# A hybrid decoder trunk on one core: two decay tables bound behind the delta branch's inputs, and one group of transposes behind its last product

## The chip, the cores and the metric

The kernel runs on one core of a Trainium2 chip. The core has a matrix engine (TensorE, PE in the profile, with its weight loads under PEld), a vector engine (VectorE, DVE), an activation engine (ScalarE, ACT), a general engine (GpSimd, POOL) and a queue engine (SyncE, SP) that issues most of the transfers. Each engine runs its own list of instructions in order, and the lists meet only in semaphores. The metric is the time of one execution in microseconds, as the median of several.

## The reference, cut to what matters

The reference has two layers. Each is a half-step feed-forward block, a token-mixing part with two branches side by side, and another half-step feed-forward block. All sizes are small in tokens (256) and large in channels (1024), in float32.

```python
for l in range(DEPTH):                                  # DEPTH = 2
    h = h + 0.5 * swiglu(rms_norm(h, ffn1_norm[l]), ffn1_w_in[l], ffn1_w_out[l])
    u = rms_norm(h, mix_norm[l])
    (z_s, xbc, dt_s, qkv, z_d, b_d, a_d, gate_s, gate_d) = jnp.split(u @ w_in[l], split_points, axis=-1)
    y_s = mamba2_branch(z_s, xbc, dt_s, ...)            # the state branch, 4 groups of 8 heads
    y_d = deltanet_branch(qkv, z_d, b_d, a_d, ...)      # the delta branch, 8 heads
    merged = (jax.nn.sigmoid(gate_s) * (y_s @ ssm_w_branch[l])
              + jax.nn.sigmoid(gate_d) * (y_d @ dn_w_branch[l]))
    h = h + merged @ w_out[l]
    h = h + 0.5 * swiglu(rms_norm(h, ffn2_norm[l]), ffn2_w_in[l], ffn2_w_out[l])
return rms_norm(h, final_norm)
```

In the state branch a chunk of 128 tokens is weighted by `cb * decay`, where `decay` is the exponential of a difference of running sums, one 128 by 128 table for each head and chunk:

```python
seg = a_cum[:, :, :, None] - a_cum[:, :, None, :]
decay = jnp.where(causal, jnp.exp(jnp.where(causal, seg, 0.0)), 0.0)
y_diag = jnp.einsum("bclsg,bclsgh,bcsghp->bclghp", cb, decay, xdt)
```

## The kernel before, in words

Every weight matrix is streamed once from memory in tiles of 128 by 1024 (`wraw`). To keep float32 accuracy at the matrix engine's fast rate, ACT rounds each tile to a high part (`whi`, L68) and DVE takes the rest (`wlo`, L71). A product then is three matmuls: high by high, high by low, low by high. There are five buffers each for `wraw`, `whi` and `wlo`; a buffer is free again when the last reader of the tile in it is done, so the preparation runs up to five tiles ahead of PE and no more.

The mixer is a list of steps, `ORDER`, in which the code is written; a scheduler that works on estimated times then lays the instructions of each engine into one list, and within that it may move an instruction ahead of an older one. The steps that the change is about are the last third of the list: `D0 S0 x10 T0 D1 x11 g110 g111 S1 x20 T1 o x21 N D2 y S2 D3 x30 x31 T2 g000 g010 g001 S3 g011 T3`.

- `Dg` is `decay(g)`: the decay table of group g, `dc`, 128 by 2048. A transfer spreads the running sums over the partitions (L1061), DVE subtracts (`dc<-dc,ac`), clips at zero (L78), ACT takes the exponential, and DVE multiplies with the masked products of the group (`dc<-dc,cbt`). Two buffers, `sA` and `sB`, alternate between the groups.
- `xgi` is `xs_unit`: a product of 48 matmuls of 256 columns into one of four accumulator banks (`xs`), and then for each of its halves a convolution of width 4: one ACT instruction that writes `ca`, three DVE instructions on `ca` (255, 254 and 253 columns, L74) that read the bank, and a Silu on ACT that writes `xsT`. The bank is free when the last of these has read it.
- `Sg` is the first part of `ssd(g)`: eight transposes of `xsT` on PE (`xsb`, L1101), then on DVE the tiles `xD`, `xdt` and `xe`. `Tg` is the rest: 32 small products with the decay table (`ydb`, L1115) and one more (`yob`), sums on DVE (`xD`, `yo`), the gating by `yz`, a Square with a sum on ACT (`jk`, `sss`), a reciprocal root on POOL (`srr`, L210), and two scalings by it on ACT (`yz<-yz,srr`).
- `g...` are gate products: 24 matmuls of 512 columns into two banks (`t0`, `t1`).
- `o` and `N` are the delta branch's end. `dn_T(hp)` transposes four heads' outputs on PE (`oT`, L1154), gates them on DVE (`og`), and splits them into a high part on ACT (`bh`) and a low part on DVE (`bl`). `dn_branch` multiplies these with the branch's weights in 96 matmuls of 512 columns (`b`, L335 to L337) into four banks, and adds to the gates (`tg`).
- `y` is `ss_T(0)`, four transposes (`yT`, L1169) of the state branch's first group, whose product follows after `T3`.

`tc.issue_after(ins)` binds the instructions that a block writes behind `ins` on the engine of `ins`, if they are on that engine. It makes no semaphore; it only fixes their place in that engine's list.

Of the kernel before, what the change touches and what calls it, by code (L numbers as in the profile page):

```python
# [11 lines left out]
ALU = mybir.AluOpType  # L12
# [4 lines left out]
P = 128  # L17
D = 1024
S = 256
# [34 lines left out]
def trunk_kernel(ctx, tc, x, wst, wsm, norms, lpar, rpar, cst, out):  # L54
    nc = tc.nc
    V, A, G, PE = nc.vector, nc.scalar, nc.gpsimd, nc.tensor
# [10 lines left out]
    def act(o, i, func=AF.Copy, **kw):  # L67
        return A.activation(out=o, in_=i, func=func, **kw)  # L68

    def tt(o, a, b, op):  # L70
        return V.tensor_tensor(out=o, in0=a, in1=b, op=op)  # L71

    def stt(o, a, s, b, op0, op1):
        return V.scalar_tensor_tensor(out=o, in0=a, scalar=s, in1=b, op0=op0, op1=op1)  # L74

    def ts(o, a, s1, op0, sc2=None, op1=None):
        if op1 is None:
            return V.tensor_scalar(out=o, in0=a, scalar1=s1, scalar2=None, op0=op0)  # L78
        return V.tensor_scalar(out=o, in0=a, scalar1=s1, scalar2=sc2, op0=op0, op1=op1)

    def f(ap):
        return ap.bitcast(F32)

    def tmp2(name):
        return s2.tile([P, 512], F32, tag="s2", name=name)

    def trb(name):
        return trp.tile([P, 512], F32, tag="tr", name=name)

    def accb(name):  # L90
        return accp.tile([P, 512], F32, tag="acc", name=name)

    def small(shape, name, bufs=2):
        return sm.tile(shape, F32, tag=name, name=name, bufs=bufs)
# [54 lines left out]
    state = {"loaded": 0, "prepped": 0, "taken": 0, "last": None, "hold": False, "behind": {}, "late": {}, "first": 0, "turns": {}, "first_chunk": False, "cap": n_forms}  # L149
# [69 lines left out]
    h = cpool.tile([P, 2, D], F32, name="h")  # L219
# [11 lines left out]
    ident = cs[:, 0:P]  # L231
# [164 lines left out]
    def out_chunks(ps, stat, ks, last, group=1, split=False, first=None):  # L396

        for g0 in range(0, len(ks), group):
            kk = ks[g0 : g0 + group]
            ws = [(k, take()) for k in kk]  # L400
            for t in range(2):
                order = [(k, n) for n in range(2) for k in range(len(kk))]
                if t == 1 and not split:
                    m = len(kk) - 2 if len(kk) == NSPL else len(kk)
                    order = [(k, n) for k in range(m) for n in range(2)]
                    order += [(k, n) for n in range(2) for k in range(m, len(kk))]
                order = [(k, n, 0, 512) for k, n in order]
                if t == 1 and split:
                    order = [o for o in order if o[1] == 0]
                    order += [(k, 1, c, c + 256) for c in (0, 256) for k in range(len(kk))]  # L410
                state["sums"] = []
                for k, n, c0, c1 in order:
                    k, (wh, wl) = ws[k]
                    sh, sl = stat(k, t)
                    c = slice(n * 512 + c0, n * 512 + c1)
                    begin = k == 0 if first is None else first and t == n == 1
                    bank = ps[t][n][:, c0:c1]
                    if c0:
                        begin, bank = k == kk[0], ps[2][:, 0:256]
                    ins = mm3(bank, sh, sl, wh[:, c], wl[:, c], begin, k == last)  # L420
                    state["sums"].append(ins)
# [171 lines left out]
    def mixer(l, nxt):  # L593
# [13 lines left out]
        yz = {}  # L607
# [37 lines left out]
        ac = small([P, 2, 40], "ac", 1)  # L645
# [380 lines left out]
        late = {}  # L1026
# [32 lines left out]
        def decay(g):  # L1059
            dc = slots.tile([P, 8, 2, P], F32, tag=("sA", "sB")[g % 2], name="dc")  # L1060
            nc.sync.dma_start(  # L1061
                dc[:].rearrange("p h t l -> p (h t l)"),
                rdram[8 * g : 8 * g + 8].rearrange("a b -> (a b)").partition_broadcast(P),
            )
            tt(
                dc[:], dc[:],
                ac[:, :, 8 * g : 8 * g + 8].rearrange("p t h -> p h t")[:, :, :, None].to_broadcast([P, 8, 2, P]),
                ALU.subtract,
            )
            dv = dc[:].rearrange("p h t l -> p (h t l)")  # L1070
            ts(dv, dv, 0.0, ALU.min)
            act(dv, dv, AF.Exp)
            tt(dc[:], dc[:], late["cbm"][:, g, None].to_broadcast([P, 8, 2, P]), ALU.mult)
            decs[g] = dc

        def xs_unit(g, i):
# [73 lines left out]
        def dn_T(hp):  # L1150
            bank = trb("oT")
            bv = bank[:].rearrange("p (a c i) -> p a c i", a=2, c=4)
            for c in range(4):
                PE.transpose(bv[:, :, c, :], vb[:, c, hp, :], ident)  # L1154
            og = tmp2("og")
            stt(og[:], bank[:], dnw, late["zdT"][:, 2 * hp : 2 * hp + 2, :].rearrange("p h t -> p (h t)"), ALU.mult, ALU.mult)
            oh = s2.tile([P, 2, S], F32R, tag="s2", name="bh")
            ol = s2.tile([P, 2, S], F32R, tag="s2", name="bl")
            act(oh[:].rearrange("p a t -> p (a t)"), og[:])
            tt(ol[:].rearrange("p a t -> p (a t)"), og[:], f(oh[:]).rearrange("p a t -> p (a t)"), ALU.subtract)  # L1160
            brT[("d", hp)] = (oh, ol)

        def ss_T(j):
            bank = trb("yT")
            g, k0 = j // 2, (j % 2) * 2
            for k in range(2):
                for t in range(2):
                    c0 = (k0 + k) * P
                    PE.transpose(bank[:, k * S + t * P : k * S + (t + 1) * P], yz[g][:, t, c0 : c0 + P], ident)  # L1169
            oh = s2.tile([P, 2, S], F32R, tag="s2", name="bh")  # L1170
            ol = s2.tile([P, 2, S], F32R, tag="s2", name="bl")
            for k in range(2):
                w = snw[:, 2 * j + k : 2 * j + k + 1]
                act(oh[:, k], bank[:, k * S : (k + 1) * S], scale=w)
                stt(ol[:, k], bank[:, k * S : (k + 1) * S], w, f(oh[:, k]), ALU.mult, ALU.subtract)
            brT[("s", j)] = (oh, ol)

        def branch(kind, n, mk, tail=1):
            ps = [[accb("b"), accb("b")] for _ in range(2)]
            held = {}  # L1180

            def stat(k, t):
                oh, ol = held[k // 2]
                return oh[:, k % 2, t * P : (t + 1) * P], ol[:, k % 2, t * P : (t + 1) * P]

            made = 1
            for j0 in list(range(n - tail)) + [n - tail]:
                js = range(j0, j0 + (tail if j0 == n - tail else 1))
                while made < min(js[-1] + 2, n):
                    mk(made)  # L1190
                    made += 1
                for j in js:
                    held[j] = brT.pop((kind, j))
                out_chunks(ps, stat, [2 * j + i for j in js for i in range(2)], 2 * n - 1, group=2 * len(js))
            return ps

        def dn_branch():
            ps = branch("d", 4, dn_T)
            m = tg[1]
            for t in range(2):  # L1200
                for n in range(2):
                    sl = slice(n * 512, (n + 1) * 512)
                    stt(m[:, t, sl], m[:, t, sl], 1.0, ps[t][n][:], ALU.add, ALU.mult)
# [5 lines left out]
        def step(name):  # L1209
# [10 lines left out]
            elif kind == "M":  # L1220
                masks()
            elif kind == "I":
                next(inv, None)
            elif kind == "R":
                next(rc, None)
            elif kind == "b":
                bcm(*num)
            elif kind == "d":
                zdm(*num)
            elif kind == "x":  # L1230
                xs_unit(*num)
            elif kind == "P":
                drain(ssd_pre())
            elif kind == "D":
                decay(*num)
            elif kind == "g":
                gate(*num)
            elif kind == "S":
                heads[num[0]] = ssd(*num)
                next(heads[num[0]])  # L1240
            elif kind == "T":
                drain(heads[num[0]])
            elif kind == "o":
                dn_T(0)
            elif kind == "y":
                ss_T(0)
            elif kind == "N":
                dn_branch()
# [33 lines left out]
    for l in range(DEPTH):  # L1282
        ffn(norm_vec(3 * l + 1))
        mixer(l, 3 * l + 2)
        add = ffn(norm_vec(3 * l + 3) if l + 1 < DEPTH else None)
# [153 lines left out]
```

## Time and profile before

| what | value |
|---|---|
| median of 3 runs | 1543.27 us (1543.04 to 1545.02) |
| the profiled execution's own time | 1541.48 us |
| its span from first to last instruction | 1539.7 us |
| granted TensorE clock | 0.999 |
| DVE busy / ACT busy | 1229.7 us (80%) / 944.8 us (61%) |
| memory read | 297.72 MB, 195 GB/s over the span |

Each row of the timeline gives the start and the length of an instruction, or of a run of equal ones, in microseconds, then the engine, the line, the operation, the tiles (written `<-` read), the sizes and the count; in brackets stands how long the engine had been idle before it, and who released it. An engine starts its next instruction a little before the former has ended, so the step from start to start is somewhat shorter than the length. The two layers run the same lists: the first layer's mixer ends its state branch at about 404 to 572 us, and the second's some 761 us later.

### The profile page before, as it was taken

The numbers are of one execution on the slowest core, as the hardware profiler recorded it, in microseconds if no ns is written. First come the engines' busy times: TensorE is split into PE (matmuls) and PEld (weight loads), VectorE is DVE, ScalarE is ACT, GpSimd is POOL, SyncE is SP. The second block draws the span as 40 slices with busy tenths as digits, with TensorE's granted clock in tenths as the row PEclk, the third lists the DMA queues.
The fourth block names the chain that finished last, engine by engine and source line by source line (L and its number), as shares of the span: only waits on it lengthen the run. The fifth ranks groups of instructions, "written<-read, shape, count | busy, mean of one in ns | idle before, by whom it ended". The sixth has DMA issues, their size and how long they took to land.

```text
span 1539.7 us, 29072 instructions
## 1 busy us (share of the span) xinstructions
PE 1522.8 (99%) x11473; PEld 1384.4 (90%) x11473; DVE 1229.7 (80%) x1859; ACT 944.8 (61%) x1532; POOL 81.8 (5%) x92
## 2 busy tenths in 40 slices
PE   8999999999999999999999999999999999999998
PEld 7999889999888888999899998899998888899997
DVE  6878769967899766789778887689589996677886
ACT  5655667765665645555555566676756666455565
POOL 0000110000000000000100012010000000000010
PEclk9999999999999999999999999999999999999999
DMA  7687775653565556587867687665345555556785
GB/s 277 190 265 231 226 228 167 187 164 111 178 213 171 163 166 196 185 256 211 261 225 225 208 253 229 197 193 180 117 141 202 179 170 186 176 177 195 247 241 156
DMA packets 98831, 305.73 MB, mean 199 GB/s; under 512 B 22837, under 2 KB 23813, under 8 KB 97670
## 3 DMA queue, kind: packets, MB, share of 16 engines
q1 hardware_dynamic: 93796, 290.95, 57.2%
q0 software_dynamic: 4608, 12.58, 5.1%
q8 instruction: 90, 1.47, 0.4%
q14 instruction: 47, 0.39, 0.1%
q10 hardware_dynamic: 290, 0.33, 0.1%
HBM read 297.72 MB, written 1.92 MB: 195 GB/s over the span
## 4 chain that ended last, share of the span: by engine, by line
PE 89%; DVE 4%; ACT 2%; DMA 2%; issue 1%; SPq 1%; POOL 0%; POOLq 0%; ACTq 0%; DVEq 0%
PE fc L346 10%; PE fc L340 9%; PE fc L345 9%; PE t L366 9%; PE o L337 4%; PE o L335 4%; PE o L336 4%; PE f L366 3%; PE b L335 3%; PE b L337 3%; PE b L336 3%; PE p L336 2%; PE p L337 2%; PE p L335 2%; PE xs L345 1%; PE xs L340 1%
## 5 line engine op out<-in xcount | busy, mean ns | idle before, releaser
L71 DVE TENSOR_TENSOR wlo<-wraw,whi 128x1024 fp32r<-128x1024 f32 x488 | 591.8, 1221 | 186.7 <-ACT whi L68 172.2
L68 ACT ACTIVATE whi<-wraw 128x1024 fp32r<-128x1024 f32 x488 | 511.6, 1059 | 271.0 <-PE fc L345 92.5
L346 PE MATMUL fc<-uW,wlo 128*128 128x256 f32 x1280 | 354.9, 277 | 0.0
L340 PE MATMUL fc<-uW,whi 128*128 128x256 f32 x1280 | 354.1, 277 | 0.0
L345 PE MATMUL fc<-uW,whi 128*128 128x256 f32 x1260 | 348.3, 276 | 0.0
L340 PEld LDWEIGHTS fc<-uW,whi 128*128 128x128 f32 x1280 | 240.5, 188 | 0.8
L346 PEld LDWEIGHTS fc<-uW,wlo 128*128 128x128 f32 x1280 | 240.5, 188 | 0.0
L345 PEld LDWEIGHTS fc<-uW,whi 128*128 128x128 f32 x1260 | 236.5, 188 | 0.8
L366 PE MATMUL t<-whi,uW 128*128 128x512 f32 x512 | 165.3, 397 | 0.0
L366 PEld LDWEIGHTS t<-whi,uW 128*128 128x128 f32 x512 | 95.9, 188 | 21.6 <-issue 1.3
L68 ACT ACTIVATE whi<-wsum 128x1024 fp32r<-128x1024 f32 x64 | 68.0, 1062 | 58.8 <-PE fc L345 32.9
L366 PE MATMUL t<-wlo,uW 128*128 128x512 f32 x256 | 100.2, 392 | 0.0
L71 DVE TENSOR_TENSOR wlo<-wsum,whi 128x1024 fp32r<-128x1024 f32 x64 | 78.2, 1221 | 7.9 <-ACT whi L68 5.6
L335 PE MATMUL b<-whi,bh 128*128 128x512 f32 x192 | 76.1, 398 | 0.3
L336 PE MATMUL b<-wlo,bh 128*128 128x512 f32 x192 | 74.9, 390 | 0.0
L337 PE MATMUL b<-whi,bl 128*128 128x512 f32 x192 | 74.2, 393 | 0.0
L340 PE MATMUL xs<-uW,whi 128*128 128x256 f32 x256 | 72.8, 284 | 0.0
L346 PE MATMUL xs<-uW,wlo 128*128 128x256 f32 x256 | 71.4, 279 | 0.0
L345 PE MATMUL xs<-uW,whi 128*128 128x256 f32 x254 | 70.6, 278 | 0.0
L335 PE MATMUL o<-whi,gh 128*128 128x512 f32 (+1 forms) x160 | 62.0, 388 | 0.0
L337 PE MATMUL o<-whi,gl 128*128 128x512 f32 (+1 forms) x160 | 61.8, 386 | 0.0
L336 PE MATMUL o<-wlo,gh 128*128 128x512 f32 (+1 forms) x160 | 61.7, 386 | 0.0
(337 smaller groups left out, 3291.7 us busy)
## 6 DMA issues: line engine op xcount, KB each, us to landing
wraw<-in_wst_dram SPq DMA_DIRECT2D x504, 512.0 KB, 4.9
wsum<-in_wst_dram SPq DMA_DIRECT2D x16, 512.0 KB, 7.3
wsum<-in_wst_dram POOLq DMA_DIRECT2D x16, 512.0 KB, 8.7
dc<-rdram SPq DMA_DIRECT2D x8, 1024.0 KB, 8.5
nw<-in_norms_dram SPq DMA_DIRECT2D x6, 512.0 KB, 5.9
h<-u POOLq DMA_DIRECT2D x12, 256.0 KB, 6.8
gb<-rdram SPq DMA_DIRECT2D x8, 256.0 KB, 5.6
h<-in_x_dram SPq DMA_DIRECT2D x4, 256.0 KB, 3.7
```

The source lines that it names most:

```text
L68: return A.activation(out=o, in_=i, func=func, **kw)
L71: return V.tensor_tensor(out=o, in0=a, in1=b, op=op)
L335: PE.matmul(ps, lh, rh, start=start, stop=False)
L336: PE.matmul(ps, lh, rl, start=False, stop=False)
L337: return PE.matmul(ps, ll, rh, start=False, stop=stop)
L340: PE.matmul(ps, wh, mh, start=start, stop=False)
L345: PE.matmul(ps, wh, ml, start=False, stop=False)
L346: PE.matmul(ps, wl, mh, start=False, stop=stop)
L366: ins = PE.matmul(ps[t][:], st, mv, start=k0 == 0 and j == 0, stop=k0 == KT - 2 and j == 5)
```

## The change

The third and the fourth group's decay table are touched: for g of 2 and 3, `decay(g)` puts its subtraction on DVE behind an instruction kept in `late["branch"]`. For the third group that is the low part of the delta branch's last heads (`bl` of hp 3); for the fourth it is the third group's last multiplication, because `decay` now also stores its own last instruction there. And the four transposes of `ss_T(0)` are bound on PE behind the last product of the delta branch.

```diff
-            tt(
-                dc[:], dc[:],
-                ac[:, :, 8 * g : 8 * g + 8]...to_broadcast([P, 8, 2, P]),
-                ALU.subtract,
-            )
+            with ExitStack() as behind:
+                if g > 1:
+                    behind.enter_context(tc.issue_after(late["branch"].ins))
+                tt(
+                    dc[:], dc[:],
+                    ac[:, :, 8 * g : 8 * g + 8]...to_broadcast([P, 8, 2, P]),
+                    ALU.subtract,
+                )
...
-            tt(dc[:], dc[:], late["cbm"][:, g, None].to_broadcast([P, 8, 2, P]), ALU.mult)
+            late["branch"] = tt(dc[:], dc[:], late["cbm"][:, g, None].to_broadcast([P, 8, 2, P]), ALU.mult)
...
-            tt(ol[:].rearrange("p a t -> p (a t)"), og[:], f(oh[:]).rearrange("p a t -> p (a t)"), ALU.subtract)
+            ins = tt(ol[:].rearrange("p a t -> p (a t)"), og[:], f(oh[:]).rearrange("p a t -> p (a t)"), ALU.subtract)
             brT[("d", hp)] = (oh, ol)
+            if hp == 3:
+                late["branch"] = ins
...
-                    PE.transpose(bank[...], yz[g][:, t, c0 : c0 + P], ident)
+                    with ExitStack() as behind:
+                        if j == 0:
+                            behind.enter_context(tc.issue_after(late["sums"].ins))
+                        PE.transpose(bank[...], yz[g][:, t, c0 : c0 + P], ident)
...
             ps = branch("d", 4, dn_T)
+            late["sums"] = state["sums"][-1]
```

The scheduler answers with another order of its own on DVE, ACT and PE from here to the end of the fourth group's part; the counts of instructions stay, but ACT's list has two loads of a function table fewer in each layer. On SP the fourth table's transfer stands one weight load later. Three places show it, all in the first layer; the second has the same.

DVE, ahead of the second group's transposes. `ca_5255` is the convolution whose Silu the last of the `xsb` transposes wait for, `dc_5754` the third group's table. Before:

```order
L71 TENSOR_TENSOR wlo_5302<-wraw_5189,whi_5301 128x1024
L74 SCALAR_TENSOR_TENSOR ca_5255<-xs_5188,lp_2175,ca_5255 128x255
L71 TENSOR_TENSOR dc_5754<-dc_5754,ac_2267 128x2048
L74 SCALAR_TENSOR_TENSOR ca_5255<-xs_5188,lp_2175,ca_5255 128x254
L71 TENSOR_TENSOR wlo_5308<-wraw_5195,whi_5307 128x1024
L74 SCALAR_TENSOR_TENSOR ca_5255<-xs_5188,lp_2175,ca_5255 128x253
```

The same place now:

```order
L71 TENSOR_TENSOR wlo_5302<-wraw_5189,whi_5301 128x1024
L74 SCALAR_TENSOR_TENSOR ca_5255<-xs_5188,lp_2175,ca_5255 128x255
L74 SCALAR_TENSOR_TENSOR ca_5255<-xs_5188,lp_2175,ca_5255 128x254
L74 SCALAR_TENSOR_TENSOR ca_5255<-xs_5188,lp_2175,ca_5255 128x253
L71 TENSOR_TENSOR wlo_5308<-wraw_5195,whi_5307 128x1024
```

The table's subtraction and one split of weights no longer stand inside the convolution. On PE all eight `xsb` transposes now stand together, where two of them stood between the matmuls of the next product.

ACT, at the start of the delta branch's products, the first of which reads `bh_5492`. `yz_2398` is the second group's gated sum, scaled by POOL's `srr_5481`; `whi_5586` is the high part of a weight tile for the branch's third pair of rows. Before:

```order
L68 ACTIVATE whi_5505<-wraw_5305 128x1024
L68 ACTIVATE jk_5478,sss_5473<-yz_2398 128x512
L68 ACTIVATE ca_5557<-xs_5496,lp_2175 128x256
L68 ACTIVATE bh_5492<-og_5490 128x512
L68 ACTIVATE xsT_5357<-ca_5426 128x256
L68 ACTIVATE yz_2398<-yz_2398,srr_5481 128x512 x2
L68 ACTIVATE whi_5586<-wraw_5359 128x1024
```

Now:

```order
L68 ACTIVATE whi_5505<-wraw_5305 128x1024
L68 ACTIVATE xsT_5357<-ca_5426 128x256
L68 ACTIVATE jk_5478,sss_5473<-yz_2398 128x512
L68 ACTIVATE ca_5557<-xs_5496,lp_2175 128x256
L68 ACTIVATE whi_5586<-wraw_5359 128x1024
L68 ACTIVATE yz_2398<-yz_2398,srr_5481 128x512 x2
L68 ACTIVATE bh_5492<-og_5490 128x512
```

`bh_5492` stood ahead of the two scalings, and now stands behind them and behind a high part.

DVE, between the third group's `xe` and the first convolution of the last `x` product. `dc_5791` is the fourth group's table, `ca_5859` the first of four convolutions on the two last `xs` banks. Before:

```order
L71 TENSOR_TENSOR xe_5789<-xdt_5777,dE_2287 128x512
L78 TENSOR_SCALAR dc_5791<-dc_5791 128x2048
L71 TENSOR_TENSOR wlo_5802<-wraw_5678,whi_5801 128x1024
L71 TENSOR_TENSOR wlo_5808<-wraw_5684,whi_5807 128x1024
L71 TENSOR_TENSOR wlo_5875<-wraw_5714,whi_5874 128x1024
L71 TENSOR_TENSOR dc_5791<-dc_5791,cbt_4930 128x2048
L74 SCALAR_TENSOR_TENSOR ca_5859<-xs_5798,lp_2175,ca_5859 128x255
```

Now:

```order
L71 TENSOR_TENSOR xe_5789<-xdt_5777,dE_2287 128x512
L71 TENSOR_TENSOR dc_5791<-dc_5791,ac_2267 128x2048
L71 TENSOR_TENSOR wlo_5802<-wraw_5678,whi_5801 128x1024
L78 TENSOR_SCALAR dc_5791<-dc_5791 128x2048
L71 TENSOR_TENSOR wlo_5808<-wraw_5684,whi_5807 128x1024
L74 SCALAR_TENSOR_TENSOR ca_5859<-xs_5798,lp_2175,ca_5859 128x255
L71 TENSOR_TENSOR wlo_5875<-wraw_5714,whi_5874 128x1024
L71 TENSOR_TENSOR dc_5791<-dc_5791,cbt_4930 128x2048
```

The fourth table's subtraction has come into this stretch; it stood some twenty instructions earlier, among the delta branch's products. The third table's multiplication, too, now stands later, right behind the second of the four `tg` sums instead of ahead of the last `og`. On PE the second gate product reads a bank that becomes free only with the convolutions that follow here, and two of the eight `xsb` transposes of the fourth group now stand ahead of that product.

More of the change, by code (lines that the diff above doesn't have):

```diff
@@ L1064, in decay @@
             )
-            tt(
-                dc[:], dc[:],
-                ac[:, :, 8 * g : 8 * g + 8].rearrange("p t h -> p h t")[:, :, :, None].to_broadcast([P, 8, 2, P]),
-                ALU.subtract,
-            )
+            with ExitStack() as behind:
[3 more added lines that the diff above has]
+                    dc[:], dc[:],
+                    ac[:, :, 8 * g : 8 * g + 8].rearrange("p t h -> p h t")[:, :, :, None].to_broadcast([P, 8, 2, P]),
+                    ALU.subtract,
+                )
             dv = dc[:].rearrange("p h t l -> p (h t l)")
@@ L1168, in ss_T @@
                     c0 = (k0 + k) * P
-                    PE.transpose(bank[:, k * S + t * P : k * S + (t + 1) * P], yz[g][:, t, c0 : c0 + P], ident)
+                    with ExitStack() as behind:
+                        if j == 0:
+                            behind.enter_context(tc.issue_after(late["sums"].ins))
+                        PE.transpose(bank[:, k * S + t * P : k * S + (t + 1) * P], yz[g][:, t, c0 : c0 + P], ident)
             oh = s2.tile([P, 2, S], F32R, tag="s2", name="bh")
```

## The prediction

> **What bounds the kernel now.** I read the page first: busy times and the chain that ended last.
>
> ```profile
> PE 1522.8 (99%) x11473; PEld 1384.4 (90%) x11473; DVE 1229.7 (80%) x1859; ACT 944.8 (61%) x1532; POOL 81.8 (5%) x92
> PE 89%; DVE 4%; ACT 2%; DMA 2%; issue 1%; SPq 1%; POOL 0%; POOLq 0%; ACTq 0%; DVEq 0%
> ```
>
> PE has matmuls in flight for 99% of the span, so only two things count: where PE stands still, and what makes it stand still anew. The change touches the end of the state branch in each layer. Next I read PE's own timeline there for idle time.
>
> ```profile
> 441.12 0.82 PE L1101 MATMUL xsb<-cs,xsT 128*128 128x128 f32 x6
> 444.59 0.44 PE L1101 MATMUL xsb<-cs,xsT 128*128 128x128 f32 x2 [0.93 <-ACT xsT L68]
> 1205.95 0.44 PE L1101 MATMUL xsb<-cs,xsT 128*128 128x128 f32 x2 [0.94 <-ACT xsT L68]
> 458.04 1.25 PE L1154 MATMUL oT<-cs,vb 128*128 128x128 f32 x10
> 459.44 0.50 PE L335 MATMUL b<-whi,bh 128*128 128x512 f32 x1
> 460.94 0.38 PE L1154 MATMUL oT<-cs,vb 128*128 128x128 f32 x2
> 1220.80 0.50 PE L335 MATMUL b<-whi,bh 128*128 128x512 f32 x1
> ```
>
> PE waits 0.93 us for the last `xsT`, and between the end of the `oT` transposes (458.04 + 1.25 = 459.29) and the first product of the delta branch it waits 0.15. The second layer is the same, 761.36 later. From here to the merge there is nothing else to win: (0.93 + 0.15) x 2 = 2.2 us is all. The windows by engine say who is full at these places (PE, PEld, DVE, ACT, POOL, clock, DMA share, GB/s):
>
> ```profile
> 441.00:460.00 19.00, 17.92 (x189) 16.59 (x188) 18.90 (x29) 13.50 (x20) 1.34 (x1) 1.00 0.64 211
> ```
>
> DVE is busy 18.90 of 19 us, and the granted clock is 1.00. What DVE does next, and what ACT does for it, sets PE here.
>
> **Part 1, the third table leaves the first convolution: a gain.** DVE and ACT ahead of the late transposes:
>
> ```profile
> 439.83 2.28 DVE L71 TENSOR_TENSOR dc<-dc,ac 128x2048 f32<-128x2048 f32 x1
> 442.03 0.47 DVE L74 SCALAR_TENSOR_TENSOR ca<-xs,lp,ca 128x254 f32<-128x254 f32 x1
> 442.42 1.22 DVE L71 TENSOR_TENSOR wlo<-wraw,whi 128x1024 fp32r<-128x1024 f32 x1
> 443.56 0.47 DVE L74 SCALAR_TENSOR_TENSOR ca<-xs,lp,ca 128x253 f32<-128x253 f32 x1
> 444.12 0.42 ACT L68 ACTIVATE xsT<-ca 128x256 f32<-128x256 f32 x1 [1.26 <-DVE ca L74]
> ```
>
> Steps from start to start are 2.20 for a table instruction, 1.14 for a `wlo`, 0.39 for a `ca`. Without the subtraction and the `wlo` in the middle, the two `ca` run at 439.83 and 440.22 and end at 440.69; ACT, busy with a high part until then, gives `xsT` by 441.35. PE comes to its eight transposes at 441.12 and needs that tile for the fourth. The 0.93 goes, and about 0.07 for breaking into the matmuls: PE is 1.0 us early from here, in each layer.
>
> **Part 2, the first product of the delta branch: a loss.** It reads `bh`. In the order now, ACT makes a `whi`, an `xsT`, `jk`, a `ca`, another `whi`, then both scalings `yz<-yz,srr`, and only then `bh`. The scalings wait for POOL, POOL for `sss` on DVE, and `sss` stands behind a `wlo` that needs the first `whi`. The rows of all these:
>
> ```profile
> 452.30 0.36 PE L340 MATMUL xs<-uW,whi 128*128 128x256 f32 x1
> 456.70 1.06 ACT L68 ACTIVATE whi<-wraw 128x1024 fp32r<-128x1024 f32 x1 [0.21 <-PE xs L345]
> 458.41 0.17 DVE L79 TENSOR_SCALAR sss<-sss 128x2 f32<-128x2 f32 x1
> 458.66 1.61 POOL L210 TENSOR_TENSOR srr<-sss,mhalf 128x2 f32<-128x2 f32 x1 [25.77 <-DVE sss L79]
> 458.76 0.62 ACT L68 ACTIVATE bh<-og 128x512 fp32r<-128x512 f32 x1
> 460.30 1.34 ACT L68 ACTIVATE yz<-yz,srr 128x512 f32<-128x512 f32 x2 [0.61 <-POOL srr L210]
> 461.55 1.04 ACT L68 ACTIVATE whi<-wraw 128x1024 fp32r<-128x1024 f32 x1
> 481.80 0.49 PE L1169 MATMUL yT<-cs,yz 128*128 128x128 f32 x3
> ```
>
> The first `whi` waits for PE to release a buffer, so it comes 1.0 earlier with PE: 455.70 to 456.76. Then `wlo` to 457.92, `sss` there; from `sss` to `yz` is 460.30 - 458.41 = 1.89, so `yz` at 459.81; the pair takes 461.55 - 460.30 = 1.25, so `bh` at 461.06; from `bh` to the first product is 459.44 - 458.76 = 0.68, so the product at **461.74**. The second `whi` and the `ca` (about 457.5 to 459.0) lie inside the wait for POOL. PE would be ready at 459.29 - 1.0 + 0.22 = 458.5: all twelve `oT` stand ahead of it now, and two cost 0.22. The stall is 3.24 us instead of 0.15. Bounds: if POOL answers 1.0 earlier than before and nothing else (yz at 459.3), 2.7; if the head start is lost on the way (yz at 460.30), 3.7. I take 3.24, since each link has its own row.
>
> The two `oT` and one `yT` that stood among the 96 products stand outside now, which gives 0.22 + 0.12 = 0.34 back; a product's step is (481.80 - 459.44 - 0.34) / 96 = 0.229. What waits behind `bh` on ACT (the other `bh`, `xsT`) is needed more than 13 products later; DVE's `bl` follows `bh` by 0.7, and PE has five products, 1.14, in hand. PE is then 461.74 - 459.44 - 0.34 = **+1.96** late at the third group's product.
>
> **Part 3, both tables meet the last convolutions: a second loss.** DVE's rows in this stretch, and what ACT and PE do beside it (the second row is the table's clip in the listing by tile, shortest, median and longest in ns):
>
> ```profile
> 481.32 0.69 DVE L74 SCALAR_TENSOR_TENSOR tg<-tg,b 128x512 f32<-128x512 f32 x1 [0.24 <-PE b L337]
> L78 DVE TENSOR_SCALAR dc<-dc x8: 1216/1220/1224, 408.3 to 1248.8; 128x2048 f32<-128x2048 f32 x8
> 497.65 0.47 DVE L74 SCALAR_TENSOR_TENSOR ca<-xs,lp,ca 128x253 f32<-128x253 f32 x1
> 498.04 0.68 DVE L71 TENSOR_TENSOR xD<-xD,ydb 128x512 f32<-128x512 f32 x1
> 498.63 0.68 DVE L71 TENSOR_TENSOR yo<-yob,eA 128x512 f32<-128x512 f32 x1
> 498.20 1.28 ACT L68 ACT_TABLE_LOAD   x1 [2.96 <-DVE ca L74]
> 499.82 1.00 ACT L68 ACTIVATE ca<-xs,lp 128x256 f32<-128x256 f32 x2
> 500.43 2.46 DVE L74 SCALAR_TENSOR_TENSOR ca<-xs,lp,ca 128x255 f32<-128x255 f32 x6
> 502.23 0.89 PE L366 MATMUL t<-whi,uW 128*128 128x512 f32 x3
> ```
>
> The second gate product needs the bank that the fifth of the six `ca` reads last: 500.43 + 4 x 0.39 + 0.47 = 502.46. Its first matmul is the third of the three at 502.23, so PE gets there at 502.7, some 0.25 later: no stall. In the new order DVE has, from the second `tg` on: 3 `tg` (as `xD`, 498.63 - 498.04 = 0.60), 2 `bl` (0.39), 5 of `xD`, `xdt`, `xe`, 6 `wlo`, 3 `ca`, and of the tables two multiplications and one subtraction (2.20 each) and one clip (1.22 less the usual overlap, 1.14): 1.8 + 0.8 + 3.0 + 6.8 + 1.2 + 4.4 + 2.2 + 1.1 = 21.3. The second `tg` starts when its bank is done, 84 products after 461.74 and 0.24 on, at 481.2, so the third `ca` ends at 502.5. Then ACT loads the Silu table and makes `xsT` and a `ca` (before: 498.13 to about 500.37, 2.24), DVE starts the six at 504.85, and the fifth ends at 506.88. PE arrives at 502.7 + 1.96 + 0.22, for two `xsb` that moved ahead, 504.9. The stall is 1.98. Those two no longer stand later, so PE leaves the stretch 506.88 - 502.7 - 0.22 = 3.95 late. Bounds: nothing, if DVE keeps its old margin; 2.2 + 2.2 - 0.25 = 4.1, if the third table's multiplication and the fourth's subtraction count whole. I take 1.98.
>
> **What costs nothing.** The tables are ready in time:
>
> ```profile
> 493.99 2.08 PE L1115 MATMUL ydb<-xdt,dc 128*64 128x64 f32 x64
> dc<-rdram SPq DMA_DIRECT2D x8, 1024.0 KB, 8.5
> 450.49 1.28 ACT L68 ACT_TABLE_LOAD   x1
> 451.78 1.92 ACT L68 ACTIVATE dc<-dc 128x2048 f32<-128x2048 f32 x1
> ```
>
> The third's multiplication ends near 484, and its product comes at 493.99 + 1.96; the fourth's ends near 500.6, and its product comes after the gate product of part 3. Were that cover gone, a table's chain, 2.28 + 1.22 + 1.28 + 1.92 + 2.28 = 9.0 us, would show on PE. The fourth table's transfer goes one weight load later on SP; it can go when the second group's product has read the buffer, about 450, lands 8.5 us later in the median, and is used at 491; that weight load gains a place. The four `yT` stay four. Two table loads like the one above go in each layer. They lay beside `xs` matmuls that ran without a gap, so I count 0. [...]
>
> **The sum.** Per layer -1.0 + 0.22 + 3.24 - 0.15 - 0.34 = 1.97, and with 1.98 it is +3.95 (its bounds: +1.4, with 2.7 and nothing, and +6.5, with 3.7 and 4.1); two layers +7.9. The profiled execution took 1541.48, so its like becomes 1549.4; the median of the runs is 1.79 above it, and becomes 1543.27 + 7.9 = 1551.2.
>
> **Rivals.**
> - B: only the first stall. If DVE finds 2 us in the stretch of part 3, 1543.27 + 2 x 1.96 = 1547.2. For it: the sum of 21 us has no slack of mine in it. Against it: it has no idle time in it either.
> - C: PE slows after the long stall. At the start of the run the array is slow after its idle time, and in the middle, after a shorter one, it is not:
>
> ```profile
> 10.64 1.83 PE L366 MATMUL f<-whi,uW 128*128 128x512 f32 x3
> 12.27 1.35 PE L366 MATMUL f<-wlo,uW 128*128 128x512 f32 x3
> 13.45 1.08 PE L366 MATMUL f<-whi,uW 128*128 128x512 f32 x4
> 1166.25 0.70 PE L1045 MATMUL cbb<-BC 128*128 128x256 f32 x2 [1.28 <-DVE vb L71]
> ```
>
>  The six matmuls from 10.64 to 13.45 take 2.81 where six take 1.37 later: 1.4 us lost. If 3.24 us of idleness do the same, two layers cost 2.9 more: 1554.1. Against it: 1.28 us did nothing, and nothing between was seen. [...]
> - D: no stall, not slower. If `bh` is done before 458.5, only the gaps go: 1543.27 - 2.3 = 1541.0. This needs `sss` at 454.7 or so (458.5 less 0.68, 1.25 and 1.89), 3.2 us before the place that the `wlo` in front of it allows; the full DVE of 441 to 460, which loses two table instructions, speaks for an earlier `sss`, the `whi` that PE releases speaks against.
>
> **How the numbers follow.** A, as summed: 0.62; B 0.14; C 0.12; D 0.08; anything else 0.04. The predicted time is A's, 1551.2. The low end, 1546.2, is the lower bound of the sum, 2 x 1.4 = 2.9 with the rounding, and takes B in; the high end, 1555.5, holds C, and A with both stalls near the middle of their upper halves. A change of 0.2%, 3.1 us, is about what a measurement of this kernel can tell from none: A and C are slower, B (+3.9) mostly, D within.
>
> **What would show it.** Right: in the profile after, no idle time at `xsb`; about 3.2 us of idle PE ahead of the first `b`, released by ACT's `bh`; about 2 us ahead of a gate product, released by DVE's `ca`, in both layers; the clock at 1.0. Wrong: a `b` that starts without a wait, or `t` matmuls of the delta branch's time at half pace (C), or a new wait at `ydb` for a table.

## The result and the profile after

The changed kernel takes 1550.39 us in the median (1549.87 to 1552.24), the kernel before 1543.28 beside it: a ratio of 1.0046, 95% interval 1.0032 to 1.006. It is slower, and the forecast of 1551.2 lies 0.8 above it. The profiled execution has a span of 1548.1, 8.4 more than before. As the rest of this document shows, two of the forecast's terms were too large and one that it left at nothing was 1.4 per layer; the total came out so close because these nearly cancel, which is luck.

The page of the changed kernel, busy times and the chain that ended last:

```profile
PE 1525.9 (99%) x11473; PEld 1386.8 (90%) x11473; DVE 1231.4 (80%) x1859; ACT 939.8 (61%) x1528; POOL 80.0 (5%) x92
PE 90%; DVE 4%; DMA 2%; ACT 2%; issue 1%; POOL 0%; SPq 0%; POOLq 0%; ACTq 0%; DVEq 0%
```

They read almost as before: the page cannot tell where 8 us went in a span of which PE is busy 99%. PE's timeline at the places of the prediction does:

```profile
441.15 1.16 PE L1104 MATMUL xsb<-cs,xsT 128*128 128x128 f32 x8
456.70 1.47 PE L1157 MATMUL oT<-cs,vb 128*128 128x128 f32 x12
460.60 0.79 PE L335 MATMUL b<-whi,bh 128*128 128x512 f32 x1 [2.43 <-ACT bh L68]
461.19 0.63 PE L336 MATMUL b<-wlo,bh 128*128 128x512 f32 x1
463.33 0.54 PE L335 MATMUL b<-whi,bh 128*128 128x512 f32 x1
463.71 0.39 PE L336 MATMUL b<-wlo,bh 128*128 128x512 f32 x1
505.59 0.38 PE L1104 MATMUL xsb<-cs,xsT 128*128 128x128 f32 x2
507.36 0.47 PE L366 MATMUL t<-whi,uW 128*128 128x512 f32 x1 [1.39 <-DVE ca L74]
1225.06 0.80 PE L335 MATMUL b<-whi,bh 128*128 128x512 f32 x1 [2.43 <-ACT bh L68]
1271.88 0.47 PE L366 MATMUL t<-whi,uW 128*128 128x512 f32 x1 [1.39 <-DVE ca L74]
```

The 0.93 at `xsb` is gone: the eight transposes stand in one row without a wait. The stall ahead of the first `b` is there, with the releaser that was named, but 2.43 long. The stall ahead of the second gate product is there too, 1.39 long, and both repeat in the second layer. The third thing is in the durations: the first `b` matmuls last 0.63 and follow each other after 0.43 (461.19, 461.62, ...) until about 463.7, and only then in 0.23. The windows of that stretch (PE, PEld, DVE, ACT, POOL, granted clock, DMA share, GB/s):

```profile
460.60:463.66 3.06, 3.06 (x7) 2.48 (x8) 3.02 (x7) 1.50 (x3) 0.00 (x0) 0.50 0.61 193
463.66:467.07 3.41, 3.41 (x16) 2.77 (x15) 2.48 (x5) 1.05 (x2) 0.00 (x0) 1.00 0.01 5
```

The granted clock is 0.50 behind the stall, and 1.00 from 463.66 on. DVE, ACT and the transfers are busier in the first window than in the second, but they are not what lowers the clock: from 441 to 460 in the kernel before, DVE was busy 18.90 of 19 us and the DMA share was 0.64, at a clock of 1.00. What the slow products cost is seen from the first of the 96 products to the `yT` transposes behind them. The first row is the changed kernel's; the other two are from a run, below, that has the same stall of 2.43 and full pace behind it (the fourth subtraction behind the third's clip):

```profile
483.93 0.60 PE L1177 MATMUL yT<-cs,yz 128*128 128x128 f32 x4
461.06 0.50 PE L335 MATMUL b<-whi,bh 128*128 128x512 f32 x1 [2.43 <-ACT bh L68]
482.98 0.60 PE L1177 MATMUL yT<-cs,yz 128*128 128x128 f32 x4
```

It is 483.93 - 460.60 = 23.33 us against 482.98 - 461.06 = 21.92, so 1.4 us. This is rival C.

The sum for one layer: from the `cbb` products behind their wait for DVE to the short wait early in the product `o` (0.31 in both) the kernel before needs 572.03 - 404.88 = 167.15, the changed one 576.24 - 404.92 = 171.32, so +4.17. From the rows: -0.93 - 0.15 + 2.43 + 1.39 + 1.4 = 4.1.

Why the first stall was shorter stands on ACT, DVE and POOL:

```profile
456.52 1.22 DVE L71 TENSOR_TENSOR wlo<-wraw,whi 128x1024 fp32r<-128x1024 f32 x1 [0.45 <-ACT whi L68]
457.66 0.16 DVE L79 TENSOR_SCALAR sss<-sss 128x2 f32<-128x2 f32 x1
457.73 0.74 DVE L74 SCALAR_TENSOR_TENSOR og<-oT,lp,zdT 128x512 f32<-128x512 f32 x1
457.90 0.69 POOL L210 TENSOR_TENSOR srr<-sss,mhalf 128x2 f32<-128x2 f32 x1 [24.98 <-DVE sss L79]
458.70 1.33 ACT L68 ACTIVATE yz<-yz,srr 128x512 f32<-128x512 f32 x2
459.93 0.62 ACT L68 ACTIVATE bh<-og 128x512 fp32r<-128x512 f32 x1
```

The chain is the one that was forecast, `wlo`, `sss`, `srr`, `yz`, `bh`, but POOL's `srr` takes 0.69 where it took 1.61 before, so from `sss` to `yz` it is 1.04 instead of 1.89. Behind `sss` DVE now runs `og`, 0.74 long; before it ran a `wlo` of 1.22:

```profile
458.49 1.22 DVE L71 TENSOR_TENSOR wlo<-wraw,whi 128x1024 fp32r<-128x1024 f32 x1
```

### The profile page after: what moved, and what is told of

Its sections match the earlier page's. It is cut to its first block, busy times and chain, and to the rows that moved or that the text cites. A ratio compares the mean times of both kernels' runs of the same rounds, so it can differ in the third digit from the quotient of the medians.

```text
span 1548.1 us, 29074 instructions
## 1 busy us (share of the span) xinstructions
PE 1525.9 (99%) x11473; PEld 1386.8 (90%) x11473; DVE 1231.4 (80%) x1859; ACT 939.8 (61%) x1528; POOL 80.0 (5%) x92
## 4 chain that ended last, share of the span: by engine, by line
PE 90%; DVE 4%; DMA 2%; ACT 2%; issue 1%; POOL 0%; SPq 0%; POOLq 0%; ACTq 0%; DVEq 0%
PE t L366 11%; PE fc L346 9%; PE fc L340 9%; PE fc L345 9%; PE o L337 3%; PE o L336 3%; PE o L335 3%; PE f L366 3%; PE b L335 3%; PE b L336 3%; PE b L337 3%; PE p L336 2%; PE p L337 2%; PE p L335 2%; PE xs L340 1%; PE xs L346 1%
```

## The experiments

Edits are against the changed kernel. Theory (T): two separate losses, the first stall with its slow products, made by `bh` standing behind the scalings, and the second stall, made by DVE's work ahead of the last convolutions. Rivals: that they are one loss in two places, that the bound transposes or ACT's table load carry part of it, and, for the pace, that the length of a stall decides it.

**The decay bindings alone.**

```diff
-                        if j == 0:
+                        if j == 99:
                             behind.enter_context(tc.issue_after(late["sums"].ins))
```

> The two bindings of the decay differences alone; the four transposes of the state branch are left to the scheduler. If the decay differences carry the whole change, the time is that of the changed kernel, 1550.4, within 1 us, with the stall of 2.4 ahead of the first b and of 1.4 ahead of a gate product in each layer. If the bound transposes carry part of it, it lies between 1543.3 and 1549.

Measured: 1550.35 (1549.35 to 1552.36), ratio to before 1.0047, 1.0033 to 1.0061. PE's rows of the first `b` and of the gate product:

```profile
460.38 0.63 PE L1177 MATMUL yT<-cs,yz 128*128 128x128 f32 x4 [0.45 <-DVE og L74]
462.36 0.50 PE L335 MATMUL b<-whi,bh 128*128 128x512 f32 x1 [1.35 <-ACT bh L68]
507.26 0.47 PE L366 MATMUL t<-whi,uW 128*128 128x512 f32 x1 [1.83 <-DVE ca L74]
```

The time is that of the whole change: the binding of the four transposes leaves it as it is. The stalls were not the expected ones: 0.45 + 1.35 ahead of the first `b`, 1.83 at the gate product, and the products were slow behind the second stall (granted clock 0.66 in the 5 us from 507.26), not the first (1.00 in the 5 us from 462.36).

**The scalings behind the first `bh`,** both in the first layer and one of two in the second. `scaled(t)` is the scaling, taken out of `ssd` for g = 1.

```diff
+            if hp == 0 and l == 1:
+                late["scaled"](0)
-            act(oh[:].rearrange("p a t -> p (a t)"), og[:])
+            first = act(oh[:].rearrange("p a t -> p (a t)"), og[:])
+            if hp == 0:
+                with tc.issue_after(first.ins):
+                    for t in range(l, 2):
+                        late["scaled"](t)
```

> The changed kernel with both of the second group's scalings of yz bound behind the first bh in the first layer, and one of the two in the second layer. If bh waits for these two and their wait for POOL, the first stall is 2.43 - 1.25 = 1.2 in the first layer and 2.43 - 0.63 = 1.8 in the second. If something else holds bh, both stay near 2.4. For the pace: twelve transposes stand ahead of each of these stalls; full pace behind both puts the point where it drops between 1.8 and 2.43, slow products behind 1.8 put it lower.

Measured, ACT in the first layer, then PE in both:

```profile
459.48 0.62 ACT L68 ACTIVATE bh<-og 128x512 fp32r<-128x512 f32 x1
460.00 1.33 ACT L68 ACTIVATE yz<-yz,srr 128x512 f32<-128x512 f32 x2
460.15 0.50 PE L335 MATMUL b<-whi,bh 128*128 128x512 f32 x1 [1.20 <-ACT bh L68]
1225.93 0.50 PE L335 MATMUL b<-whi,bh 128*128 128x512 f32 x1 [1.82 <-ACT bh L68]
```

1.20 and 1.82 where 1.2 and 1.8 were expected: the scalings hold `bh`, and each costs its own time (1.82 - 1.20 = 0.62). The pace is full behind both (granted clock 1.00 in the 5 us from 460.15 and from 1225.93). One execution took 1548.25. The second stall was 1.26 and 1.39, hardly another than in the changed kernel:

```profile
505.37 0.47 PE L366 MATMUL t<-whi,uW 128*128 128x512 f32 x1 [1.26 <-DVE ca L74]
```

In the first layer the stretch from `cbb` to `o` is 1.50 longer than before the change, where the whole change made it 4.17 longer: 1.2 of the first stall and the 1.4 of slow pace are gone, and nothing came back at the second.

**An extra multiplication behind `sss`,** in the first layer only:

```diff
-            ts(ss[:], ss[:], 1.0 / 512.0, ALU.mult, EPS, ALU.add)
+            mean = ts(ss[:], ss[:], 1.0 / 512.0, ALU.mult, EPS, ALU.add)
...
+            if g == 1 and l == 0:
+                with tc.issue_after(mean.ins):
+                    for _ in range(2):
+                        tt(xd[0][:], xd[0][:], xd[1][:], ALU.mult)
```

> In the first layer alone, two extra multiplications xD<-xD,xD (128x512, two operands in SBUF, 0.68 each) are bound behind the second group's sss on DVE; one of them comes right behind it. If a POOL instruction waits for a DVE instruction with two SBUF operands that began before it (1.61 beside wlo, 0.69 without), srr takes about 1.07 in the first layer (it ends 0.56 after that multiplication) and 0.69 in the second, and the first stall is 0.4 longer in the first layer, 2.8. If srr is short for another reason, it stays 0.69 in both layers and the stalls are alike.

Measured, POOL and DVE in the first layer, then POOL in the second, and PE's first `b` in both:

```profile
458.20 0.68 DVE L71 TENSOR_TENSOR xD<-xD 128x512 f32<-128x512 f32 x1
458.37 1.07 POOL L210 TENSOR_TENSOR srr<-sss,mhalf 128x2 f32<-128x2 f32 x1 [24.97 <-DVE sss L79]
1221.95 0.70 POOL L210 TENSOR_TENSOR srr<-sss,mhalf 128x2 f32<-128x2 f32 x1 [25.05 <-DVE sss L79]
461.38 0.50 PE L335 MATMUL b<-whi,bh 128*128 128x512 f32 x1 [2.74 <-ACT bh L68]
1224.65 0.50 PE L335 MATMUL b<-whi,bh 128*128 128x512 f32 x1 [2.43 <-ACT bh L68]
```

1.07 against 0.70, and 2.74 against 2.43, in one execution. POOL ends 0.56 after the DVE instruction (458.20 + 0.68 + 0.56 = 459.44), as it ended 0.56 after the `wlo` before the change (458.49 + 1.22 + 0.56 = 460.27). The execution took 1548.94. So the length of `srr` goes with what DVE runs beside it: 0.69 beside `og`, 1.07 beside the extra multiplication, 1.61 beside a `wlo`. That is the first of the two outcomes; what in the DVE instruction makes it so, this run does not show.

**The third table alone.** `if g > 1:` becomes `if g == 2:`, and the transposes are left free. The fourth table's subtraction then goes directly ahead of `sss`.

> Only the third table's subtraction is bound behind the delta branch's inputs; the fourth's is free and moves up to directly ahead of the second group's sss on DVE, where a high part's remainder stood. If the wait for sss, POOL and the scalings makes the first stall, it is longer here than 2.43, since the subtraction takes 2.2 and its table lands late: 3 to 5 us, slow products behind it again, and a time of 1550 to 1556 although DVE has less to do at the last convolutions. If the stall came from the amount of DVE's work in both tables, binding one table gives about half of the loss, 1546 to 1547.

Measured: 1557.13 (1555.13 to 1557.98), ratio 1.0087, 1.0071 to 1.0104, a little above the range. DVE's and PE's rows:

```profile
461.29 2.29 DVE L71 TENSOR_TENSOR dc<-dc,ac 128x2048 f32<-128x2048 f32 x1 [3.31 <-DMA dc<-rdram]
463.50 0.16 DVE L79 TENSOR_SCALAR sss<-sss 128x2 f32<-128x2 f32 x1
464.37 1.12 PE L1177 MATMUL yT<-cs,yz 128*128 128x128 f32 x4 [4.28 <-DVE og L74]
466.38 0.79 PE L335 MATMUL b<-whi,bh 128*128 128x512 f32 x1 [0.89 <-ACT bh L68]
```

DVE waits 3.31 for the fourth table's transfer, everything behind it waits with it, and the products are slow afterwards (granted clock 0.50 in the 5 us from 466.38). There is no second stall here. It is the place of an instruction in DVE's list that costs, not the number of tables that move: half of the change costs more than the whole.

**The fourth subtraction behind the third's clip** instead of its multiplication:

```diff
-            ts(dv, dv, 0.0, ALU.min)
+            late["branch"] = ts(dv, dv, 0.0, ALU.min)
-            late["branch"] = tt(dc[:], dc[:], late["cbm"]..., ALU.mult)
+            tt(dc[:], dc[:], late["cbm"]..., ALU.mult)
```

> The changed kernel with the fourth table's subtraction bound behind the third table's clip rather than its multiplication, so that it leaves the DVE stretch ahead of the last convolutions (one 2.2 us instruction and one clip fewer there). If DVE's work makes the second stall, it goes, 1.39 per layer: 1550.4 - 2.8 = 1547.6, the first stall and the slow products as they are. If the table load on ACT and its wait set the six ca, the second stall stays and the time is 1550.4.

Measured: 1547.92 (1545.35 to 1548.98), ratio 1.0031, 1.0021 to 1.0041. The six `ca` start at 501.87 instead of 505.14, and PE goes through the gate product without a wait:

```profile
501.87 2.46 DVE L74 SCALAR_TENSOR_TENSOR ca<-xs,lp,ca 128x255 f32<-128x255 f32 x6
504.64 0.38 PE L1104 MATMUL xsb<-cs,xsT 128*128 128x128 f32 x2
504.77 0.47 PE L366 MATMUL t<-whi,uW 128*128 128x512 f32 x1
```

DVE's work makes the second stall; the table load is still there (at 499.64, 1.28 long) and does not make PE wait. The first stall is 2.43 in both layers; in the profiled execution slow products follow it in the second layer only (granted clock 0.66 in the 5 us from 1222.93, 1.00 from 461.06).

**`bh` ahead of the scalings by an earlier step,** with the second group's scalings bound behind it:

```diff
-x11 g110 g111 S1 x20 T1 o x21 ...
+x11 g110 g111 S1 x20 o T1 x21 ...
+                with ExitStack() as behind:
+                    if g == 1:
+                        behind.enter_context(tc.issue_after(late[("bh", 0)].ins))
-                act(yv, yv, scale=rr[:, t : t + 1])
+                    act(yv, yv, scale=rr[:, t : t + 1])
```

> The changed kernel with the first oT transposes one step earlier and the second group's two scalings of yz bound behind the first bh, so that bh waits no longer for POOL. If the stall ahead of the first b costs 2.43 of waiting and some 1.2 of slow pace per layer, the time falls by 2 x 3.6 = 7.2 to about 1543.2, with the second stall near 1.4 still there and no slow products. If PE's lead is only handed on to the second stall (DVE's stretch there is not moved by it), the first stall is gone, the second one grows by up to 3.6, and the time stays above 1548.

Measured: 1552.37 (1549.31 to 1553.55), ratio 1.0055, 1.0036 to 1.0073. Nothing was won. PE at the last convolutions, and DVE some 40 us ahead:

```profile
503.24 0.44 PE L1104 MATMUL xsb<-cs,xsT 128*128 128x128 f32 x2 [1.10 <-ACT xsT L68]
505.93 0.47 PE L366 MATMUL t<-whi,uW 128*128 128x512 f32 x1 [2.25 <-DVE ca L74]
467.57 3.50 DVE L71 TENSOR_TENSOR wlo<-wraw,whi 128x1024 fp32r<-128x1024 f32 x3 [2.52 <-ACT whi L68]
```

There is no wait at the first `b` at all, yet the second stall has grown from 1.39 to 1.10 + 2.25, and the slow products now stand behind it (granted clock 0.66 in the 5 us after 505.93). From 467.57 to the six `ca` the only pause of DVE over 0.3 is one of 0.81. PE comes to these two transposes 3.45 earlier than in the changed kernel (502.14 for 505.59), DVE to the six `ca` only 1.46 earlier (503.68 for 505.14), so PE waits longer for the same work. T's picture of two separate losses holds only as far as DVE can follow. In the changed kernel DVE has pauses of 0.70, 1.38, 1.63, 0.40 and 0.67 between the first `b` and the six `ca`, 4.78 in all; with the scalings moved it used some of them up (2.03 were left), came to the six `ca` at 503.16, 1.98 earlier, and the two losses came off separately. Here its list is nearly full from 467.57 on, and taking away the rest of the first stall only lengthened the second.

**Both edits.**

> Both of these at once. If the two stalls and the slow pace are the whole loss and each is removed by its own edit, 1543.2 - 2.8 = 1540.4, below the kernel before by 0.2%. If a lead of PE is lost again at the last convolutions, it is not below 1543.

Measured: 1544.31 (1542.82 to 1545.89), ratio 1.0008, 0.9999 to 1.0017. Stalls of 1.01 and 0.30 were left at the gate product, so it is not the 1540.4 of the sum. DVE still waited 2.53 for `whi` at 466.3, with the third table's subtraction held back behind the last `bl`, at 474.60.

**Both edits, with the third subtraction behind an earlier `bl`:** the third (`hp == 2`) or the second (`hp == 1`).

```diff
-            if hp == 3:
+            if hp == 2:
                 late["branch"] = ins
```

> The kernel with both edits (e7), and the third table's subtraction bound behind the third of the four bl instead of the fourth, so that it falls into the 2.5 us in which DVE waited for ACT (466.3 to 468.8 in e7's trace), and the fourth's subtraction some 8 us earlier. If DVE's work in the stretch ahead of the last convolutions sets the second stall (1.02 + 0.30 per layer left in e7), it goes, and the time falls by 2.6 to about 1541.7, 0.1% below the kernel before. If the Silu table's load and the ca on ACT set it, the stall stays and the time is e7's, 1544.3.

> The same, bound behind the second of the four bl: DVE has the third table's subtraction and clip done among the delta branch's inputs. If the earlier start only helps DVE's later stretch, the time is that of the binding behind the third bl, about 1541.7. If the 2.2 us instruction holds up the og and bl of the delta branch behind it, a new stall shows inside the 96 products, up to 2.2 per layer, and the time is 1543 to 1546.

Measured: behind the third 1540.4 (1539.11 to 1541.67), ratio 0.9983, 0.9974 to 0.9992; behind the second 1540.0 (1538.68 to 1542.09), ratio 0.998, 0.9971 to 0.9988. They are 1.3 and 1.7 below what was expected. Both are faster than both kernels of the case, by about 0.2% against the one before, with intervals that leave out 1. Behind the third `bl`, DVE and PE:

```profile
465.10 2.28 DVE L71 TENSOR_TENSOR dc<-dc,ac 128x2048 f32<-128x2048 f32 x1
467.70 2.36 DVE L71 TENSOR_TENSOR wlo<-wraw,whi 128x1024 fp32r<-128x1024 f32 x2 [0.32 <-ACT whi L68]
441.54 1.18 PE L1104 MATMUL xsb<-cs,xsT 128*128 128x128 f32 x8
457.66 0.47 PE L335 MATMUL b<-whi,bh 128*128 128x512 f32 x1
```

The subtraction fills DVE's pause (0.32 is left of 2.53), and from `cbb` to `o` PE has no wait over 0.15 in either layer. That stretch takes 571.37 - 405.32 = 166.05 and 166.05, against 167.15 and 167.04: -1.1 and -1.0 per layer, which is the gain of part 1 standing alone. The binding behind the second `bl` did not hold up the delta branch's inputs.

**The scalings behind `bh`, with the two table edits** (the transposes where the change has them):

> The changed kernel with both scalings of yz bound behind the first bh (the transposes where the change has them), the fourth's subtraction behind the third's clip, and the third's behind the third bl. The first stall is 1.2 per layer, as with the scalings alone, with full pace behind it; the second stall is gone if DVE's work sets it: per layer -0.93 - 0.15 - 0.12 + 1.2 = 0.0, a time of 1543 to 1544. If the shift of the table hurts the delta branch's inputs, it is above 1545.

Measured: 1542.12 (1541.33 to 1544.71), ratio 0.9996, 0.9987 to 1.0005. The first stall is 1.21 in both layers with full pace behind it (0.23 from one product to the next), the second is gone; 1 us below the expected range, and no different from before.

**A later bank release,** for the pace. In the second half of `x30`'s convolution:

```diff
+            if ti == 45:
+                for _ in range((3, 6)[l]):
+                    stt(ca[:], ps, 0.0, ca[:], ALU.mult, ALU.add)
```

> The changed kernel with three (first layer) and six (second layer) extra additions of zero in the second half of x30's convolution, each 0.39, so that the bank that the second gate product waits for comes free 1.2 and 2.4 later. That makes stalls of about 2.6 and 3.8 right behind products. If the length of the stall alone decides the granted pace, the products behind both are slow (0.43 a step for some 3 us). If the transposes ahead of the first b count as idle time (1.47 + 2.43 = 3.9), the stall of 2.6 is followed by full pace (0.23) and only the one of 3.8 by slow products.

Measured: the stalls became 3.87 and 5.06, since other instructions slipped in between, and half pace followed both (granted clock 0.50 in the 3.4 us from 511.45 and from 1281.12); so this pair does not tell the two theories apart. The two first stalls of the same execution do. Windows of 3.42 us behind each, first and second layer:

```profile
462.04:465.46 3.42, 3.42 (x8) 2.63 (x9) 3.38 (x7) 1.50 (x3) 0.00 (x0) 0.53 0.48 162
1232.12:1235.54 3.42, 3.42 (x15) 2.84 (x16) 3.38 (x7) 1.50 (x3) 0.00 (x0) 1.00 0.48 157
```

Both follow a stall of 2.43 behind twelve transposes, and one has 8 matmuls at a clock of 0.53, the other 15 at 1.00. Neither the length nor the transposes decide, and DVE, ACT and the transfers do not either: they are as busy in the one window as in the other (DVE 3.38 us, ACT 1.50, the transfers a share of 0.48). One execution took 1559.97.

## Why the prediction was right, and where it was not

- **Part 1, the gain of 1.0 at `xsb`: right.** The gap is gone, and where no new stall follows, the layer is 1.0 to 1.1 shorter.
- **Part 2, 3.24 ahead of the first `b`: the mechanism was right, the size was not.** 2.43. The step that failed is "from `sss` to `yz` is 460.30 - 458.41 = 1.89", taken from a row in which POOL stood beside a `wlo`. In the new order `og` follows `sss`, and the same step took 1.04. With it the product came 1.14 sooner than forecast (460.60 for 461.74), and PE was ready 0.3 sooner (458.17 for 458.5). The lower bound of 2.7 stood on `yz` at 459.3, with POOL as slow as before; `yz` came at 458.70.
- **Part 3, 1.98 ahead of the gate product: right in place and releaser, 1.39 in size.** The `ca` released PE 0.48 later than was forecast (507.36 for 506.88), and PE was there 1.07 later (505.97 for 504.9): it began its products 1.14 sooner, lost 1.4 in the slow ones, and took 11.48 instead of 11.07 for the 96 matmuls of `x30` and `x31`. The rest is small, among it 0.12 that the working gave back for a `yT`, although all four still stand ahead of `x30`. The part also counted its loss as separate from part 2's. With the scalings moved that was so (1.20 and 1.26); with the earlier `bh` it was not: with the first stall away the second was 3.35.
- **The sum, +3.95 per layer: near the measured +4.17 by luck.** 3.95 - 0.81 - 0.59 + 1.4 = 3.95: two terms were too large by 1.4 together, and 1.4 was left out.
- **Rival C, given 0.12, is what happened** on top of A, and cost 1.4 per layer, as priced. The products at half pace are one of the prediction's own signs that it is wrong. What was said against C, that 1.28 of idleness did nothing, was true (in the kernel before, the clock was 1.00 in the 5 us from 1166.25) and proved too little: a stall of 2.43 was followed by half pace, a clock of 0.50, in some places and by 1.00 in others.
- **What costs nothing: right for the tables and their loads.** No `ydb` waits for a table, and with less of DVE's work ahead of the convolutions the gate product does not wait for ACT's load. The third table alone shows the price of a table that lands late: 3.31 of DVE's time, and all that stands behind it.
- **The bound transposes: right at nothing,** as the decay bindings alone had the time of the whole.

## What to carry to other kernels

An instruction bound behind another is priced by two lists: what it now stands ahead of on its own engine, and which engine's pause it left empty. Before two stalls in a row on one engine are added up, look at the pauses that the releaser of the second has between them. As long as it could use them (4.78 us in the changed kernel), the first stall came off on its own; where its list was full (one pause of 0.81 with the earlier `bh`), removing more of the first only lengthened the second, and the gain came from starting the releaser's work in a pause it already had (the 2.53 at 466.3). And a duration taken from a row is one beside its neighbours (1.61 beside a `wlo`, 0.69 beside `og`): where the order changes, look at what runs beside it now.

## What the hardware showed that was not expected

**The granted clock fell behind some stalls and stayed full behind longer ones.** The windows below are the 5 us behind four stalls of the first layer: 2.43 ahead of the first `b` in the changed kernel, 2.43 there with the fourth subtraction behind the clip, 2.74 there with the extra multiplication, and 1.83 ahead of the gate product with the decay bindings alone.

```profile
460.60:465.60 5.00, 5.00 (x16) 4.01 (x17) 4.27 (x9) 2.55 (x5) 0.00 (x0) 0.70 0.38 121
461.06:466.06 5.00, 5.00 (x22) 4.13 (x23) 4.27 (x9) 2.56 (x5) 0.00 (x0) 1.00 0.31 111
461.38:466.38 5.00, 5.00 (x22) 4.13 (x23) 4.66 (x10) 2.02 (x4) 0.00 (x0) 1.00 0.33 109
507.26:512.26 5.00, 5.00 (x15) 4.00 (x16) 5.00 (x10) 2.48 (x7) 0.00 (x0) 0.66 0.32 102
```

The mean clock was 0.66 behind 1.83 and 1.00 behind 2.74. The slow stretch need not begin where the stall ends. With the fourth subtraction behind the clip, the second layer's stall of 2.43 ends at 1222.93; the clock is 1.00 for another 1.42, then 0.50 for 3.41, then 1.00 again:

```profile
1222.93:1224.35 1.42, 1.42 (x6) 1.20 (x7) 1.42 (x3) 0.88 (x2) 0.00 (x0) 1.00 0.66 182
1224.35:1227.76 3.41, 3.41 (x10) 2.67 (x9) 2.73 (x6) 1.66 (x3) 0.00 (x0) 0.50 0.28 106
1227.76:1231.17 3.41, 3.41 (x16) 2.78 (x16) 1.77 (x3) 1.53 (x3) 0.00 (x0) 1.00 0.00 0
```

Where the third table was bound alone, behind stalls of 4.28 and 0.89 in the first layer, the slow stretch was longer. The clock was 0.50 in two windows that overlap, from 464.37 to 471.38, and the products kept the slow step until 472.5 (472.09 to 472.52 is 0.43, 472.52 to 472.77 is 0.25):

```profile
464.37:469.37 5.00, 4.11 (x11) 3.12 (x12) 4.48 (x7) 3.09 (x6) 0.07 (x1) 0.50 0.31 105
466.38:471.38 5.00, 5.00 (x12) 3.94 (x13) 5.00 (x9) 1.39 (x3) 0.00 (x0) 0.50 0.45 132
472.09 0.61 PE L336 MATMUL b<-wlo,bh 128*128 128x512 f32 x1
472.52 0.41 PE L337 MATMUL b<-whi,bl 128*128 128x512 f32 x1
472.77 0.39 PE L335 MATMUL b<-whi,bh 128*128 128x512 f32 x1
```

What decides whether the clock falls behind a stall, and for how long, these runs do not show.

**A POOL instruction of two columns took 0.69, 1.07 or 1.61 us** by what DVE did beside it (`og`, the extra multiplication, a `wlo`), and here it stood between PE and its next product.
